# First mixer of a two-layer decoder trunk: seven block products in place of eight from the third channel block on

## The chip, the core and the metric

The kernel runs on one core of a Trainium2 chip. The metric is the device time of one execution in microseconds (us), from the first to the last instruction and what little lies around them; lower is better. The kernel before was timed three times: 1878.28, 1880.44 and 1884.79 us, a median of 1880.44 us.

## What is computed

The input x has 2048 positions of 1024 channels, in float32. The work, cut to what matters here:

```python
# layer 0: gated short convolution ("mixer")
h = rmsnorm(x, norm_a)
u = h @ w_in_a                                  # (2048,1024) @ (1024,4096)
B, C, X, G = split(u, 4)
y = B * conv3(C * X)                            # causal, width 3, per channel
x = x + (y * silu(G)) @ w_out_a
# shared keys and values, then layer 1: stick-breaking attention, 8 heads of 64
k, v = split(rmsnorm(x, norm_kv) @ w_kv, 2)
q, g = split(rmsnorm(x, norm_b) @ w_in_b, 2)
o = attention(q, k, v)                          # strictly causal, products of sigmoids, no softmax
x = x + (o * silu(g)) @ w_out_b
out = rmsnorm(x, norm_f)
```

## The kernel before

**Tiles.** x is held transposed and with its positions reversed (xT): channels lie on the 128 partitions, in KD = 8 blocks, and positions run along the free axis in 4 chunks c of CH = 512. Every product of a weight block with a chunk accumulates in one PSUM bank of 128x512.

**Three matmuls for one.** A float32 operand is split into a high part of type fp32r and a low part, the rest of it (`split`, L174: ScalarE casts the high part, VectorE or GpSimd subtracts it from the source). `mm3` (L203) multiplies high by high, high by low and low by high: 24 matmuls for an output block with the 8 channel blocks of the contraction.

**The mixer.** `mixer_in(cs)` (L277) loops over 8 output channel blocks cb, and for each over the chunks cs and the four gates C, X, B, G, so 4 x 24 matmuls for each cb and chunk. `mixer_in((0, 1))`, called m01, does the first two chunks together, so that each weight block is loaded and split once for both (`load_w`, L183, which also stores the split weights to DRAM for the chunks 2 and 3). Its normalisation is late: the matmuls run on x times the gain, and the factor 1/rms (`late_rms`, L250, tiles rs) is multiplied in behind them. Behind the matmuls of a chunk and cb: C is copied out by ScalarE (L318), multiplied with X (L325) and with the square of 1/rms (L331), put through the convolution (L338, L339, L341), multiplied with B (L343), and with the sigmoid of G, G itself and 1/rms (L348 to L354). The result goes to DRAM (y_d) and is fetched again by `proj_out`.

**Beside m01.** `stats_x` (L220) computes 1/rms of the chunks 2 and 3, 8 loads, 8 squares and 7 additions each. `fold_gains` (L360) goes through 16 blocks of the weights w_kv and w_in_b: each half block is loaded, multiplied by its gain (L368, VectorE), split (L176) and stored (L371).

**Order.** The program's generators (`mixer_in`, `proj_first`, `attention_chunk` and others) are merged by hand with weights (`merge`, `take`, the last lines of the kernel): m01 runs alone for a quarter of one chunk's work, then it is merged with the statistics and the folds, and afterwards the output projection of chunk 0 (`proj_out`, tiles po) is merged with the mixer of chunk 2, and so on. A list scheduler then puts the instructions into a fixed order on each engine; each engine runs its list in that order, and an instruction that waits holds what is behind it. DMAs are issued by SyncE (SP) in the same manner.

**Buffers.** Split weights lie in NWB = 4 tiles of 128 x 2 x 8 x 128 (whl), raw weights in NRAW = 2 tiles (wraw). The tags w, R, wth, wtl, q2, kt, vv, ot, hl and og belong to the attention and the projections, and are free or nearly free during m01.

Of the kernel before, what the change touches and what calls it, by code (L numbers as in the profile page):

```python
# [8 lines left out]
F32 = mybir.dt.float32  # L9
# [12 lines left out]
NR, NW, NT, NL, NWB, NRAW, NA, NWTS = 5, 8, 4, 5, 4, 2, 16, 2  # L22
# [7 lines left out]
NB = 3  # L30
GRP, GRY, SLACK = 3, 6, 8
# [14 lines left out]
def kernel(  # L46
# [117 lines left out]
    def square_into(acc, src, first, nm, eng=nc.vector, early=False):  # L164
        if first:
            nc.scalar.activation(acc, src, AF.Square)
        else:

            tag = "wth" if early else "t"
            sq = sb.tile([P, CH], F32, name=f"sq_{nm}", tag=tag, bufs=NT if tag == "t" else NWTS)  # L170
            nc.scalar.activation(sq, src, AF.Square)
            eng.tensor_add(acc, acc, sq)
# [5 lines left out]
    def w_tile(nm, kt=KD):  # L178
        return sb.tile([P, 2, kt, P], F32R, name=f"whl_{nm}", tag="whl", bufs=NWB)
# [4 lines left out]
    def load_w(src, key, nm, kt=KD, eng=nc.vector):  # L184

        if key not in split_d:
            wt = w_tile(nm, kt)
            raw = sb.tile([P, kt, P], F32, name=f"wr_{nm}", tag="wraw", bufs=NRAW)
            nc.sync.dma_start(out=raw, in_=src.rearrange("(k p) n -> p k n", p=P))
            split(wt[:, 0], wt[:, 1], raw, eng)  # L190
            split_d[key] = dram.tile([P, 2, kt, P], F32, name=f"sw_{nm}")
            nc.sync.dma_start(out=split_d[key], in_=wt.bitcast(F32))
            return wt
        wt = w_tile(nm, kt)
        nc.sync.dma_start(out=wt.bitcast(F32), in_=split_d[key])
        return wt
# [6 lines left out]
    def mm3(ps, wts, a, kt=KD):  # L203

        hi, lo = wts[:, 0], wts[:, 1]
        n = 0
        for k in range(kt):
            for w, m in ((hi, 0), (hi, 1), (lo, 0)):
                ins = nc.tensor.matmul(ps, w[:, k, :], a[k][:, m, :], start=n == 0, stop=n == 3 * kt - 1)  # L209
# [11 lines left out]
    def load_x(c, k, nm):  # L221
        x = ld512(f"x{nm}_{c}_{k}")
        nc.sync.dma_start(out=x, in_=xT[k * P:(k + 1) * P, cols(c)])
        return x

    def norm_x_late(c, between=None):

        hc, xs = [], []
        for k in range(KD):
            if k == 1 and between is not None:  # L230
                between()
            tag, bufs = (("w", NW), ("R", NR) if k < NR else ("ld", NL))[c]
# [11 lines left out]
    def squares(c, xs):  # L244
        acc = sb.tile([P, CH], F32, name=f"acc_h{c}", tag="acc", bufs=2)
        for k, x in enumerate(xs):
            square_into(acc, x, k == 0, f"h{c}{k}", nc.gpsimd, early=True)
        return acc

    def late_rms(c, y):  # L250
        pb = bcast(y, f"h{c}")
        r = sb.tile([P, CH], F32, name=f"rs_{c}", tag="w", bufs=NW)
        nc.scalar.copy(r, pb)
        r2 = sb.tile([P, CH], F32, name=f"rs2_{c}", tag="w", bufs=NW)
# [3 lines left out]
    rx = {}  # L258

    def stats_x(c):  # L260

        acc = sb.tile([P, CH], F32, name=f"acc_h{c}", tag="acc", bufs=2)
        for k in range(KD):
            square_into(acc, load_x(c, k, "s"), k == 0, f"h{c}{k}", early=True)
        y = const.tile([P, 4], F32, name=f"rx_{c}")
        rx[c] = rstd(acc, f"h{c}", y)
        yield 1.0

    def norm_x(c):
        hc = []  # L270
        pb = bcast(rx[c], f"hb{c}")
        for k in range(KD):
            x = load_x(c, k, "n")
# [8 lines left out]
    late_acc, late = {}, {}  # L282

    def mixer_in(cs):
# [3 lines left out]
        for cb in range(KD):  # L288
            wts = {}
            for c in cs:  # L290
# [5 lines left out]
                def gate(g, i):  # L296
                    if c not in h:
                        if c == 0:
                            load_first = lambda: wts.update({g: load_w(w_src(i), (g, cb), f"{g}{cb}_{cs[0]}")})
                            h[c], late_acc[c] = norm_x_late(c, load_first)  # L300
                        else:
                            h[c], xs = norm_x_late(c)
                            late_acc[c] = rstd(squares(c, xs), f"h{c}")
# [43 lines left out]
                if c in late:  # L347
                    nc.vector.tensor_mul(sg, pG, late[c][0])  # L348
                    nc.scalar.activation(sg, sg, AF.Sigmoid)
                    nc.vector.tensor_mul(t, t, late[c][1])  # L350
# [3 lines left out]
                nc.vector.tensor_mul(t, t, pG)  # L354
                nc.sync.dma_start(out=y_d[c][cb], in_=t)
                yield rest(24)


    def fold_gains():

        for nm, src, gain in (("kv", w_kv, gains["kv"]), ("b", w_in_b[0], gains["b"])):
            for i in range(KD):
                split_d[nm, i] = dram.tile([P, 2, KD, P], F32, name=f"sw_{nm}{i}")
                for j in range(0, KD, 4):
                    hi, lo = (sb.tile([P, 4, P], F32R, name=f"fold{m}_{nm}{i}_{j}", tag="og", bufs=KD) for m in range(2))
                    raw = lo.bitcast(F32)
                    nc.sync.dma_start(out=raw, in_=src[j * P:(j + 4) * P, i * P:(i + 1) * P].rearrange("(k p) n -> p k n", p=P))
                    nc.vector.tensor_mul(raw, raw, gain[:, j:j + 4].unsqueeze(2).to_broadcast([P, 4, P]))  # L368
                    split(hi, lo, raw)
                    for m, t in enumerate((hi, lo)):  # L370
                        nc.sync.dma_start(out=split_d[nm, i][:, m, j:j + 4, :], in_=t.bitcast(F32))  # L371
                yield 1.0
# [3 lines left out]
    def proj_out(c):  # L376

        y = []
        for k in range(KD):
            y.append(act_tile(f"y_{c}", k))  # L380
            t = ld512(f"yr_{c}_{k}")
# [27 lines left out]
    def proj_k(c, kb):  # L409
        wts = load_w(None, ("kv", kb), f"k{c}_{kb}")  # L410
# [9 lines left out]
    def proj_q(c, qb):  # L420
        wts = load_w(None, ("b", qb), f"q{c}_{qb}")
# [7 lines left out]
    def proj_v(c, vb):  # L429
        wts = load_w(None, ("kv", 4 + vb), f"v{c}_{vb}")  # L430
# [12 lines left out]
    def proj_g(c, gb):  # L443
        wts = load_w(None, ("b", 4 + gb), f"gg{c}_{gb}")
# [175 lines left out]
    def out_b_last(c):  # L620
# [3 lines left out]
        for ob in range(KD):  # L624
# [3 lines left out]
            yield from mm3(ps, wts, og, kt=3)  # L628
# [10 lines left out]
        for ob in range(KD):  # L639
            ps = lin(f"pol_{ob}")  # L640
            yield from mm3(ps, wl[ob // 4][:, :, ob % 4:ob % 4 + 1, :], og[3:4], kt=1)
# [88 lines left out]
    run(take(m01, TA / 4))  # L730
# [48 lines left out]
```

## Time and profile before

The page shows one execution, profiled.

| | |
|---|---|
| profiled execution, its own time | 1879.31 us |
| its span, first to last instruction | 1877.6 us |
| median of three runs | 1880.44 us |
| m01: its last matmul is followed by the first of `proj_out` at | 369.3 us |
| matmuls in the whole kernel, as the profile counts them | 8312 |
| mean granted TensorE clock | 0.979 |

In the rows below PE is TensorE's matmuls, PEld its weight loads, DVE VectorE, ACT ScalarE, POOL GpSimd and SP SyncE. A row of a group gives line, engine, operation, tiles and shape, then the count, the busy time in us with the mean of one in ns, and the idle time of that engine just before them. A row of the timeline gives start and duration in us. A row by windows gives the busy time of each engine in the stretch, then the granted clock, the busy share of the DMA engines, and GB/s.

### The profile page before, as it was taken

The page shows a single profiled execution, that of the slowest core. Times are in us where ns is not written, and L with a number is a line of the kernel's source. Part 1 is how long each engine was busy: PE and PEld are TensorE (multiplying, and loading weights), DVE is VectorE, ACT ScalarE, POOL GpSimd, SP SyncE. Part 2 cuts the span into 40 slices and gives each one's busy share as a digit, 9 for nine tenths or more (in the row PEclk, how much of TensorE's full clock was granted, in tenths as well). Part 3 has the DMA queues.
Part 4 walks back from the last instruction along what each step waited for, and adds up shares of the span by engine and source line. Part 5 has one row for each costly group of instructions (what it writes and reads, how often), then busy time and mean ns, then how long its engine had stood idle before and what let it go on. Part 6 is the DMA issues. An engine that isn't in the chain of part 4 may idle for free.

```text
span 1877.6 us, 24951 instructions
## 1 busy us (share of the span) xinstructions
PE 1771.9 (94%) x8312; PEld 1447.6 (77%) x8312; DVE 1261.9 (67%) x1927; ACT 772.7 (41%) x1497; POOL 450.4 (24%) x822
## 2 busy tenths in 40 slices
PE   7999999999999999999999999999988998988783
PEld 5888888888778878887888888888766886866562
DVE  7876534554243364478785478787858889889984
ACT  6423212231232143345443244454535556556642
POOL 5100000101111032132221122232223214547543
PEclk9999999999999999999999999999999999999896
DMA  9999865697978798867677766566586667778763
GB/s 292 309 324 332 307 195 165 209 328 280 336 250 281 227 330 257 290 207 250 216 253 244 248 195 204 183 215 198 180 300 196 223 194 265 260 238 278 225 196 130
DMA packets 238480, 460.44 MB, mean 245 GB/s; under 512 B 18448, under 2 KB 133136, under 8 KB 213776
## 3 DMA queue, kind: packets, MB, share of 16 engines
q1 hardware_dynamic: 178272, 400.09, 63.0%
q10 hardware_dynamic: 59920, 58.74, 10.9%
q8 instruction: 66, 1.08, 0.2%
q14 instruction: 62, 0.51, 0.1%
q0 software_dynamic: 160, 0.02, 0.1%
HBM read 322.73 MB, written 136.05 MB: 244 GB/s over the span
## 4 chain that ended last, share of the span: by engine, by line
PE 74%; DVE 10%; DMA 7%; issue 4%; ACT 2%; POOL 2%; SPq 0%; ACTq 0%; POOLq 0%; DVEq 0%
PE pX L209 9%; PE pB L209 9%; PE po L209 9%; PE pG L209 9%; PE pC L209 8%; PE wt L526 4%; PE pv L209 4%; PE pk L209 3%; PE pq L209 3%; DVE R L514 3%; PE pg L209 3%; PE av L536 3%; PE av L535 2%; PE z L500 2%; PE z L501 2%
## 5 line engine op out<-in xcount | busy, mean ns | idle before, releaser
L514 DVE TENSOR_TENSOR_SCAN R<-R,R,ones 128x512 f32<-128x512 f32 x192 | 255.0, 1330 | 25.2 <-ACT R L503 24.7
L503 ACT ACTIVATE R<-z 128x512 f32<-128x512 f32 (+1 forms) x320 | 174.0, 544 | 185.0 <-PE z L501 72.7
L176 DVE TENSOR_TENSOR wtl<-wt,wth 128x512 fp32r<-128x512 f32 (+1 forms) x320 | 186.2, 601 | 79.9 <-ACT wth L175 76.8
L175 ACT CAST wth<-wt 128x512 fp32r<-128x512 f32 (+1 forms) x320 | 159.6, 528 | 184.7 <-PE wt L526 150.3
L518 DVE TENSOR_TENSOR w<-w,R 128x512 f32<-128x512 f32 (+1 forms) x320 | 207.7, 658 | 19.6 <-POOL R L511 2.1
L209 PE MATMUL pC<-h,whl_C 128*128 128x512 f32 x768 | 189.8, 396 | 11.0 <-ACT whl_C L175 8.0
L513 POOL COPY R<-R 128x1 f32<-128x1 f32 x192 | 117.4, 613 | 340.9 <-DVE R L514 308.6
L209 PE MATMUL po<-y,whl_o 128*128 128x512 f32 x768 | 189.2, 393 | 2.4 <-DVE x L394 2.0
L209 PE MATMUL pX<-h,whl_X 128*128 128x512 f32 x768 | 186.3, 392 | 1.3 <-DVE cv L354 1.3
L209 PE MATMUL pB<-h,whl_B 128*128 128x512 f32 x768 | 185.9, 392 | 0.0
L209 PE MATMUL pG<-h,whl_G 128*128 128x512 f32 x768 | 185.7, 392 | 0.0
L526 PE MATMUL wt<-ident,w 128*128 128x128 f32 x1088 | 176.8, 278 | 7.5 <-DVE w L518 4.5
L209 PEld LDWEIGHTS pC<-h,whl_C 128*128 128x128 f32 x768 | 143.5, 189 | 44.1 <-ACT whl_C L175 8.0
L505 ACT ACTIVATE w<-z 128x512 f32<-128x512 f32 (+1 forms) x320 | 172.1, 543 | 2.5 <-PE wt L526 2.4
L209 PEld LDWEIGHTS pX<-h,whl_X 128*128 128x128 f32 x768 | 143.5, 188 | 31.5 <-DVE cv L354 1.5
L209 PEld LDWEIGHTS po<-y,whl_o 128*128 128x128 f32 x768 | 142.7, 188 | 32.1 <-DVE x L394 2.2
L209 PEld LDWEIGHTS pB<-h,whl_B 128*128 128x128 f32 x768 | 143.5, 188 | 29.7
L209 PEld LDWEIGHTS pG<-h,whl_G 128*128 128x128 f32 x768 | 143.6, 188 | 29.5
L526 PEld LDWEIGHTS wt<-ident,w 128*128 128x128 f32 x1088 | 137.4, 143 | 36.0 <-DVE w L518 6.9
L536 PE MATMUL av<-wtl,vv 128*128 128x512 f32 (+1 forms) x320 | 127.3, 401 | 27.0 <-DVE wtl L176 26.5
L514 DVE TENSOR_TENSOR_SCAN R<-R,ones 128x512 f32<-128x512 f32 (+3 forms) x128 | 116.4, 915 | 37.0 <-POOL R L509 32.8
L500 PE MATMUL z<-kt,q 128*128 128x512 f32 (+1 forms) x320 | 129.3, 406 | 5.7 <-ACT w L505 2.8
(172 smaller groups left out, 2685.1 us busy)
## 6 DMA issues: line engine op xcount, KB each, us to landing
whl_o<-sw_o SPq DMA_DIRECT2D x24, 1024.0 KB, 5.3
kt<-k_d ACTq DMA_DIRECT2D x80, 256.0 KB, 4.0
vv<-v_d ACTq DMA_DIRECT2D x80, 256.0 KB, 3.7
whl_C<-sw_C SPq DMA_DIRECT2D x16, 1024.0 KB, 5.9
whl_X<-sw_X SPq DMA_DIRECT2D x16, 1024.0 KB, 5.3
whl_B<-sw_B SPq DMA_DIRECT2D x16, 1024.0 KB, 5.8
whl_G<-sw_G SPq DMA_DIRECT2D x16, 1024.0 KB, 5.3
whl_k<-sw_kv SPq DMA_DIRECT2D x16, 1024.0 KB, 7.0
```

The costliest lines, as they stand in the source:

```text
L175: nc.scalar.copy(hi, src)
L176: eng.tensor_sub(lo, src, hi.bitcast(F32))
L209: ins = nc.tensor.matmul(ps, w[:, k, :], a[k][:, m, :], start=n == 0, stop=n == 3 * kt - 1)
L500: nc.tensor.matmul(ps[:, lom:CH], q2[:, 0, qi * P:(qi + 1) * P], kt[:, lom:CH], start=True, stop=False)
L501: nc.tensor.matmul(ps[:, lom:CH], q2[:, 1, qi * P:(qi + 1) * P], kt[:, lom:CH], start=False, stop=True)
L503: nc.scalar.activation(R[:, lo + 1:CH + 1], ps[:, lo:CH], AF.Sigmoid, scale=-0.125)
L505: nc.scalar.activation(w[:, lo:CH], ps[:, lo:CH], AF.Sigmoid, scale=0.125)
L513: nc.gpsimd.tensor_copy(R[:, 0:1], carry[qi])
L514: nc.vector.tensor_tensor_scan(out=R[:, lo + 1:CH + 1], data0=R[:, lo + 1:CH + 1], data1=ones[:, 0:1].to_broadcast([P, CH - lo]), initial= ...
L518: nc.vector.tensor_mul(w[:, lo:CH], w[:, lo:CH], R[:, lo:CH])
L526: nc.tensor.transpose(wt[:, qi * P:(qi + 1) * P], ws[qi][:, kb * P:(kb + 1) * P], ident)
L536: ins = nc.tensor.matmul(av[:, 0:n], vs, wl[:, 0:n], start=False, stop=final)
```

## The change

The channel blocks 0 and 1 of m01 (NPL = 2) stay as they were, except that 1/rms and not its square is multiplied in once for G and once for B, with a SiLU of ScalarE in place of sigmoid and product. From block 2 on, `mixer_fast` takes two gates at a time, C with X, and B with G: the 2x2 blocks are two gates, two halves of the contraction (Q = 4 channel blocks each) and two chunks. A "unit" is one cb and one pair of gates; there are 12 of them. Each does 7 products of 12 matmuls (three for each of 4 channel blocks) where there were 8, in the form of Strassen's scheme with 4 sums on each side:

- operands, once: both chunks of x are normalised in place (16 multiplications, L420 and L430), 16 differences are taken by GpSimd, and 7 operands of 4 tiles are split; the low parts of one of them (t4) by GpSimd, of the others by VectorE;
- weights, for each unit: 4 raw halves are loaded (L464), 4 sums and differences are formed, two by VectorE and two by GpSimd, and 8 half blocks are split, the low parts of two (s3, s4) by GpSimd;
- results, for each unit: four partial results are copied from PSUM by ScalarE (`keep`), and three additions by VectorE put the outputs together. The bank `fa` collects products 1, 2, 3 and the last one, with a copy in between.

```diff
-NR, NW, NT, NL, NWB, NRAW, NA, NWTS = 5, 8, 4, 5, 4, 2, 16, 2
+NR, NW, NT, NL, NWB, NRAW, NA, NWTS = 5, 8, 4, 5, 8, 4, 16, 2
...
+    def fast_operands():
+        x0, x1 = x_in[1], x_in[0]
...
+        operand("b11", x0[:Q], [(w2, w2)] * Q)
+        for k in range(Q):
+            nc.gpsimd.tensor_sub(x0[k], x1[k], x0[k])
...
+        operand("t1", x0[:Q], [(hs[2 * k], hs[2 * k + 1]) for k in range(Q)])
...
+    def fast_weights(n, cb, gs):
...
+            sp(key, raw)
...
+            if key == "a22":
+                nc.vector.tensor_add(a22, a21, a22)
+                sp("s1", a22)
+                nc.gpsimd.tensor_sub(a21, a11, a21)
+                nc.vector.tensor_sub(a11, a22, a11)
+                sp("s2", a11)
+        nc.gpsimd.tensor_sub(a12, a12, a11)
+        sp("s4", a12, nc.gpsimd)
+        sp("s3", a21, nc.gpsimd)
...
+            yield product(a, w["a11"], "b11", True, False)
+            c0 = keep(f"f1_{nm}", a)
+            yield product(d, w["s1"], "t1", True, False)
+            p5 = keep(f"f5_{nm}", d)
...
+                yield last_product(n - 1)
+            yield product(a, w["s2"], "t2", False, False)
+            c1 = keep(f"f2_{nm}", a)
+            yield product(d, w["s4"], "b22", False, True)
+            nc.vector.tensor_add(c1, c1, d)
...
+                yield product(c, w["a12"], "b21", True, True)
+                nc.vector.tensor_add(c0, c0, c)
+            yield product(a, w["s3"], "t3", False, False)
+            x1 = keep(f"f3_{nm}", a)
+            nc.vector.tensor_add(x1, x1, p5)
...
-    run(take(m01, TA / 4))
-    merge((m01, 1.75 * TA), (chain(iter((DLY,)), stats_x(2), stats_x(3), fold_gains()), 18.0 + DLY))
+    run(take(m01, TA / 2))
+    merge((m01, 1.3 * TA), (chain(iter((DLY,)), stats_x(2), stats_x(3), fold_gains([(n, i) for i in range(8) for n in ("kv", "b")]), stats_end()), 26.0 + DLY))
```

Split weights now lie in half blocks (8 tiles of half the size) everywhere, so each load, split and store of a full block is two instructions on halves. The statistics and the folds start after channel block 1, not within block 0, and their loads are tied to a matmul that precedes them (`follow`), so that they are spread over the stretch. The result of chunk 0 and block 7 is split on the spot (`y_last`) and does not go through DRAM.

More of the change, by code (lines that the diff above doesn't have):

```diff
@@ L287, in mixer_in @@
             yield YN * 24 * MM
-        for cb in range(KD):
+        for cb in range(KD if len(cs) == 1 else NPL):
             wts = {}
+            if cb == NPL - 1 and len(cs) > 1:
+                fast_operands()
             for c in cs:
```

271 lines of the change are left out of this document (217 added, 54 removed).

## The prediction

> **What bounds the kernel now.** I read the page first, then the stretches by windows, then the chain of work in order of time, and last what TensorE waited for.
>
> ```profile
> PE 1771.9 (94%) x8312; PEld 1447.6 (77%) x8312; DVE 1261.9 (67%) x1927; ACT 772.7 (41%) x1497; POOL 450.4 (24%) x822
> ```
> ```profile
> 28.00:106.40 78.40, 77.17 (x343) 63.68 (x344) 64.49 (x122) 35.45 (x55) 14.22 (x14) 1.00 0.92 317
> 106.40:369.40 263.00, 263.00 (x1169) 218.22 (x1169) 140.85 (x212) 65.72 (x91) 12.80 (x27) 1.00 0.75 250
> ...
> 1440.00:1877.60 437.60, 368.62 (x1743) 290.75 (x1741) 372.98 (x532) 240.31 (x470) 188.80 (x259) 0.93 0.69 222
> ```
> ```profile
> 100.96 5.44 PE pG L209 x24
> 106.40 5.44 PE pC L209 x24
> ...
> 363.99 5.44 PE pG L209 x24
> 369.43 5.45 PE po L209 x24
> ```
>
> TensorE is busy 94% of the span. The change touches the work of m01 alone, and m01 ends at 369.4 us, where the first matmul of the output projection (po) stands in the chain. Its channel blocks 0 and 1 are done at 106.4 us; from there to 369.4 us TensorE is busy in 263.00 of 263 us, at a granted clock of 1.00. The chain is nothing but outputs of 24 matmuls at 5.44 us each, 226.7 ns a matmul. In this stretch time is matmuls, and VectorE has slack: 140.85 us busy of 263.
>
> **The change part by part.** My sum is made against the profiled execution: 1879.31 us (span 1877.6), 1.1 us under the median of 1880.44, so I carry the same number over to the median.
>
> *TensorE.* The stretch had 6 blocks x 2 chunks x 4 gates x 24 = 1152 matmuls, and gets 12 units x 7 x 12 = 1008, on the same tile shapes, each with its own weight load as before. 144 fewer at 226.7 ns is **-32.6 us**: 228.5 us for the products instead of 261.1 (the rest of the 263 is statistics, which stay, so 231 in all). The rest of the program keeps its matmuls.
>
> *What VectorE gets in exchange.* Its durations:
>
> ```profile
> 42.56 1.22 DVE L176 TENSOR_TENSOR whl_G<-wr_G,whl_G 128x1024 fp32r<-128x1024 f32 x1
> 43.70 1.22 DVE L176 TENSOR_TENSOR whl_C<-wr_C,whl_C 128x1024 fp32r<-128x1024 f32 x1
> ...
> 49.70 0.75 DVE L341 SCALAR_TENSOR_TENSOR cv<-p,cw,cv 128x512 f32<-128x512 f32 x1
> 50.37 0.69 DVE L172 TENSOR_TENSOR acc_h<-acc_h,sq_h 128x512 f32<-128x512 f32 x1
> 50.97 0.68 DVE L343 TENSOR_TENSOR cv<-cv,pB 128x512 f32<-128x512 f32 x1
> 51.57 0.69 DVE L348 TENSOR_TENSOR sg<-pG,rs 128x512 f32<-128x512 f32 x1
> ```
>
> From start to start a 128x512 TENSOR_TENSOR takes 0.60 us, with a scalar as third input 0.67, and a 128x1024 one 1.14. A pair of units (one channel block) holds 12 low parts, 4 sums of weights, 6 additions of products, and 6 + 4 instructions of convolution and gating: 28 x 0.60 + 4 x 0.67 = 19.5 us, 117 us for six blocks. The folds and statistics, partly done before 106 us until now, fall into the stretch whole: 64 + 14 instructions, 46.8 us. Small ones for the statistics, and the first output weights and y ahead of po: some 13 us. Together **177 us** where 231 are to be had.
>
> *GpSimd, and its quarrel with VectorE.* The stretch gets 48 differences and low parts for the weights, 8 for t4 and 2 for y: 58 of 128x512. Before, such ones ran at the start of the kernel:
>
> ```profile
> 11.55 1.28 POOL L172 TENSOR_TENSOR acc_h<-acc_h,sq_h 128x512 f32<-128x512 f32 x1 [0.59 <-ACT sq_h L171]
> ...
> 26.07 8.75 POOL L172 TENSOR_TENSOR acc_h<-acc_h,sq_h 128x512 f32<-128x512 f32 x5 [0.27 <-ACT sq_h L171]
> ```
> ```profile
> 26.81 1.75 DVE L239 SCALAR_TENSOR_TENSOR h<-xh,g_a,h 128x512 fp32r<-128x512 f32 x1
> ...
> 29.09 2.89 DVE L239 SCALAR_TENSOR_TENSOR h<-xh,g_a,h 128x512 fp32r<-128x512 f32 x2
> ...
> 31.97 1.70 DVE L239 SCALAR_TENSOR_TENSOR h<-xh,g_a,h 128x512 fp32r<-128x512 f32 x1
> 33.60 1.25 DVE L134 TENSOR_SCALAR t_h<-v_h 128x4 int32<-128x4 int32 x1
> ```
>
> Alone, GpSimd takes 1.28 us. Five in a row beside a busy VectorE take 1.75 each, and VectorE's own, 0.75 us as at 49.70, take 1.75, 1.45 twice and 1.70; a tiny one of 128x4 takes 1.25. These five cost VectorE about 1.0 + 1.4 + 0.95 + 1.1 = 4.4 us, 0.9 each, though VectorE had work at every moment. I take **0.8** for one, since some will fall into VectorE's waits; the ends are 0 (all of them do) and 1.28 (each whole). 58 x 0.8 = 46 us, so VectorE needs 177 + 46 = **223 of 231 us**, 97%. GpSimd itself, at 58 x 1.75 = 102 us, is far from full.
>
> The Trainium skill's page "SBUF — State Buffer", section "Who interferes with whom", says that a VectorE instruction with two SBUF inputs and a GpSimd instruction that reads SBUF exclude each other, and that whoever comes second blocks until the other is through. The rows above agree as far as they go; taken to the letter it is the upper end of 1.28 us, and the second rival below is what that end gives.
>
> *How much TensorE waits.* At 97% the two engines are level, and each waits for the other by turns. Two stretches of before bracket it: from 28 to 106.4 us VectorE was 82% busy (64.49 of 78.40) and TensorE lost 1.2 us; from 1440 us on VectorE was 85% busy, and TensorE idle for 69 of 437.6 us (16%), above all for VectorE:
>
> ```profile
> PE av L536 <- DVE wtl L176: 24.1, 21, 2.7
> ```
>
> The second stretch is attention, with short steps to and fro; weights here are split about one unit (19 us) ahead, which is nearer to the first. I take a little over 4% of 231, **+10 us**; ends 0 and 16%, 37 us.
>
> *Entry.* VectorE can't normalise the second chunk before its rs is there:
>
> ```profile
> 67.20 0.69 DVE L331 TENSOR_TENSOR p<-p,rs 128x512 f32<-128x512 f32 x1 [1.91 <-ACT rs L255]
> ```
>
> In the changed order that is again before TensorE's 216th matmul or so. From there 57 instructions (35.1 us) and 13 of GpSimd's (10.4 us at 0.8) lie ahead of the last low part of b21, so 67.2 + 45.5 = 112.7 us. TensorE asks for b21 behind its first two products, at 106.4 + 5.4 = 111.8. That is 1 us late, with 0 and 1.28 for the contention from 0 to 7; I take **+2**.
>
> *Exit.* po's first matmul needs y_0, which VectorE splits behind y_7, and y_7 hangs on the last unit's third product.
>
> ```profile
> L349 ACT ACTIVATE sg<-sg 128x512 f32<-128x512 f32 x15 | 9.5, 630 | 28.9 <-DVE sg L348 28.9
> L318 ACT COPY cs<-pC 128x512 f32<-128x512 f32 x16 | 9.3, 581 | 26.0 <-PE pC L209 26.0
> ...
> L175 ACT CAST y<-yr 128x512 fp32r<-128x512 f32 x8 | 5.0, 622 | 6.3 <-PE pG L209 4.5 <-DMA yr<-y_d 1.5
> ```
>
> Copy, addition, SiLU, product, cast, low part, then y_0: 0.58 + 0.60 + 0.63 + 0.60 + 0.62 + 0.60 + 0.60 and 0.6 of small work is 4.8 us, of which the last product (12 matmuls, 2.7 us) hides 2.7. **+2**, ends 0 and 5 (two instructions of GpSimd's in the way).
>
> *At nothing.* ScalarE gets 16 weight casts, 8 copies, 2 scalings and 2 SiLUs a block, 28 x 0.62 = 17 of 38 us, and the folds' casts; TensorE's other products hide it unless ScalarE is held behind a late VectorE, which the +10 holds. The halved loads move the same bytes, but double SyncE's issues; each is prefetched, and another load in flight hides it.
>
> Sum: -32.6 + 10 + 2 + 2 = -18.6 us; 1879.3 - 18.6 = 1860.7, **1861 us**.
>
> **The rivals.**
>
> *All is hidden.* If contention falls into VectorE's waits (0 in place of 0.8: 177 of 231, 77% busy, less than the 82% that cost 1.2 us above), only TensorE's sum counts: 1879.3 - 32.6 = **1847**. For it: between 106.4 and 369.4 us nothing at all held TensorE. Against: the five instructions above.
>
> *VectorE becomes the bound, slower than before.* If each of the 58 costs VectorE its whole 1.28 us, that is 74, and 177 + 74 = 251 us. VectorE's list is fixed, and it also stands still for the folds' loads:
>
> ```profile
> DVE fold_b L368 <- DMA fold_b<-in_w_in_b_dram: 22.2, 13, 3.2
> ...
> DVE fold_kv L368 <- DMA fold_kv<-in_w_kv_dram: 4.6, 4, 2.1
> ```
>
> With 22 of these 27 us, VectorE takes 273, against the old 263: 1879.3 + 10 = **1889**. It decides from the price x at which 177 + 58x + 22 > 263, that is x = 1.1 us. Against: 0.9 measured with VectorE never free.
>
> *Late folds.* At 0.8, and with the folds' 27 us of waits on top of 223, VectorE needs 250, 19 more than TensorE; with entry and exit, -32.6 + 19 + 4 = -9.6: **1870**. The loads speak for it:
>
> ```profile
> xs<-in_xT_dram SPq DMA_DIRECT2D x16, 256.0 KB, 6.3
> fold_kv<-in_w_kv_dram SPq DMA_DIRECT2D x16, 256.0 KB, 6.2
> ```
> ```profile
> 35.49 0.68 DVE L368 TENSOR_TENSOR fold_kv<-fold_kv,g_kv 128x512 f32<-128x512 f32 x1
> ...
> 103.76 0.69 DVE L368 TENSOR_TENSOR fold_kv<-fold_kv,g_kv 128x512 f32<-128x512 f32 x1 [1.31 <-DMA fold_kv<-in_w_kv_dram]
> ```
>
> The stretch moved 250 GB/s x 263 us = 66 MB at a DMA share of 0.75. Some 11 MB of it that were moved before 106 us (16 loads for the statistics, 4 MB, and 9 half folds, the two rows above and seven between, of 0.75 MB with their stores) come in, 77 MB in 231 us, 330 GB/s; the stretch from 28 us on did 317 at 0.92. Against: the change paces those loads, and GpSimd's work that falls into these waits costs nothing.
>
> **How the numbers follow.** Forecast, 1852 to 1866 us: 0.45. All hidden: 0.20. Late folds: 0.20. VectorE the bound: 0.15. The range takes in all but the worse part of the last and the little below all hidden: 1845 to 1883. About 0.3% (5.6 us) is what a measurement of this kernel can tell from no change. Faster by more: 0.45 + 0.20 + 0.13 of the late folds = 0.78; within: the other 0.07; slower: 0.15.
>
> **What would show it.** In the changed profile the first po starts near 351 us (369.4 - 18.6); near 337 all was hidden, beyond 369 VectorE is the bound. In the Strassen stretch VectorE should be busy over 90%, its low parts of the weights should average 0.8 us or more instead of 0.69, and TensorE's waits should be many small ones, released by VectorE or by casts of ScalarE that follow it, 14 us in all; a matmul should still be 226.7 ns. Long waits of VectorE for fold loads would speak for the late folds. From po on the time should be as before, within 5 us; if it differs by more, the halved weight tiles or the new order there did something that I left out.

## The result and the profile after

The changed kernel takes **1910.58 us**, the median of four runs (1910.32 to 1919.14), beside 1882.62 us for the kernel before on the same chip (four runs, 1878.28 to 1889.84): a ratio of 1.0151, 95% interval 1.0124 to 1.0179. It is slower by about 28 us, where 1861 was forecast and the range ended at 1883. Its profiled execution is the longest of its four, 1919.14 us with a span of 1917.4, 8.6 us over the median; what is said of places goes by that execution.

First its page, the row of busy time:

```profile
PE 1773.5 (92%) x8168; PEld 1433.6 (75%) x8168; DVE 1346.4 (70%) x2039; ACT 834.3 (44%) x1650; POOL 552.1 (29%) x890
```

The 144 matmuls are gone (8168 for 8312), and yet TensorE is busy 1.6 us longer than before. The first matmul of the output projection (po) shows what became of the stretch; second row, the stretch by windows, from 106.4 us to there (PE, PEld, DVE, ACT, POOL busy, then clock, DMA share, GB/s):

```profile
L217 PE MATMUL po<-y,whl_o x115: 387/389/797, 382.8 to 419.7; 128*128 128x512 f32 x115
```
```profile
106.40:382.80 276.40, 248.78 (x1037) 196.67 (x1035) 218.82 (x315) 129.28 (x235) 104.76 (x83) 0.97 0.82 269
```

po starts at 382.8 us, not at 369.3 as before and not at 351 as forecast. VectorE's busy time, 218.82 us, is what I had worked out (223), but in 276 us and not in 231. TensorE is idle for 27.6 us there. What it waited for, and below it what ScalarE waited for in the same stretch (total, times, longest):

```profile
PE fa_C L489 <- ACT f_C L499: 8.0, 7, 2.1
PE fa_B L489 <- ACT f_B L499: 6.1, 7, 1.6
PE po L217 <- ACT y L176: 5.3, 1, 5.3
PE fd_B L489 <- ACT whl_s_B L176: 3.1, 1, 3.1
```
```profile
ACT fold_kv L176 <- DVE fold_kv L590: 22.2, 12, 4.0
ACT fold_b L176 <- DVE fold_b L590: 17.0, 9, 3.4
ACT whl_s_C L176 <- POOL fr_C L476: 13.3, 5, 4.3
ACT whl_s_B L176 <- POOL fr_B L476: 11.6, 5, 3.0
ACT sq_h L172 <- DMA xs<-in_xT_dram: 11.0, 6, 2.9
```

TensorE is not released by VectorE but by ScalarE, which is busy 129 of 276 us: its copy of a bank (`keep`, L499), or its cast, stands in its list behind casts that wait. They wait for three things: the folds (VectorE's product, which waits for a load), GpSimd's sums of weights, and the loads of the statistics. One chain in the timeline (start, duration), ScalarE and then TensorE:

```profile
172.17 0.61 ACT L176 CAST whl_a_B<-fr_B 128x512 fp32r<-128x512 f32 x1
177.50 0.63 ACT L169 ACTIVATE acc_h<-xs 128x512 f32<-128x512 f32 x1 [4.72 <-DMA xs<-in_xT_dram]
178.03 0.60 ACT L176 CAST whl_s_B<-fr_B 128x512 fp32r<-128x512 f32 x1
```
```profile
178.69 0.73 PE L489 MATMUL fd_B<-op_t,whl_s_B 128*128 128x512 f32 x2 [3.15 <-ACT whl_s_B L176]
179.26 4.54 PE L489 MATMUL fa_B<-op_b,whl_a_B 128*128 128x512 f32 x12
183.64 2.65 PE L489 MATMUL fa_C<-op_t,whl_s_C 128*128 128x512 f32 x11
```

A square of the statistics, which nobody needs for 200 us, waits 4.72 us for its load, and the cast that TensorE needs stands behind it. The row below the wait shows a second loss: 12 matmuls take 4.54 us in place of the usual 2.9.

And GpSimd beside VectorE, the rows of the changed stretch for the low parts and sums that each makes (count, busy us, mean ns), with the same sums on VectorE in the run below without GpSimd:

```profile
L177 POOL TENSOR_TENSOR whl_s_C<-fr_C,whl_s_C 128x512 fp32r<-128x512 f32 x12 | 19.7, 1658 | 4.0 <-ACT whl_s_C L176 4.0
L476 POOL TENSOR_TENSOR fr_C<-fr_C,fr_C 128x512 f32<-128x512 f32 x6 | 12.1, 2014 | 28.1 <-DVE whl_a_C L177 28.1
```
```profile
L177 DVE TENSOR_TENSOR fold_kv<-fold_kv,fold_kv 128x512 fp32r<-128x512 f32 x16 | 13.4, 840 | 1.4 <-ACT fold_kv L176 1.4
L177 DVE TENSOR_TENSOR whl_s_B<-fr_B,whl_s_B 128x512 fp32r<-128x512 f32 x12 | 10.5, 876 | 4.8 <-ACT whl_s_B L176 4.4
```
```profile
L476 DVE TENSOR_TENSOR fr_C<-fr_C,fr_C 128x512 f32<-128x512 f32 x6 | 4.1, 682 | 0.0
```

The same sum takes GpSimd 2014 ns and VectorE 682, and VectorE's own low parts grow from 0.69 to 0.84 and 0.88 us in the two groups shown (the other groups of low parts lie between 0.68 and 0.83, but for those of the operands at the entry, of which the last section speaks).

### The profile page after: what moved, and what is told of

The parts are those of the page before. It is cut to its first block, busy times and chain, and to the rows that moved or that the text cites. A ratio compares the mean times of both kernels' runs of the same rounds, so it can differ in the third digit from the quotient of the medians.

```text
span 1917.4 us, 25511 instructions
## 1 busy us (share of the span) xinstructions
PE 1773.5 (92%) x8168; PEld 1433.6 (75%) x8168; DVE 1346.4 (70%) x2039; ACT 834.3 (44%) x1650; POOL 552.1 (29%) x890
## 4 chain that ended last, share of the span: by engine, by line
PE 57%; DVE 14%; DMA 9%; issue 7%; POOL 3%; ACT 2%; SPq 1%; POOLq 0%; ACTq 0%; DVEq 0%
PE po L217 8%; PE pX L217 5%; PE wt L757 4%; PE pv L217 4%; PE pC L217 4%; PE pB L217 4%; PE pk L217 4%; PE pG L217 4%; PE pq L217 3%; DVE R L745 3%; PE pg L217 3%; PE av L767 3%; PE av L766 2%; PE z L731 2%; PE z L732 2%
## 5 line engine op out<-in xcount | busy, mean ns | idle before, releaser
L744 POOL COPY R<-R 128x1 f32<-128x1 f32 x192 | 107.3, 560 | 360.2 <-DVE R L745 317.4
L217 PE MATMUL pC<-h,whl_C 128*128 128x512 f32 x480 | 124.6, 402 | 10.4 <-ACT whl_C L176 6.8
L740 POOL TENSOR_SCALAR_AFFINE_SELECT R<-R 128x128 f32<-128x128 f32 x128 | 56.8, 444 | 267.7 <-ACT R L734 265.3
L731 PE MATMUL z<-kt,q 128*128 128x512 f32 (+1 forms) x320 | 128.7, 405 | 4.9 <-ACT w L736 4.7
L766 PE MATMUL av<-wth,vv 128*128 128x512 f32 (+1 forms) x320 | 122.5, 383 | 8.1 <-ACT wth L176 7.6
L217 PE MATMUL pX<-h,whl_X 128*128 128x512 f32 x480 | 122.6, 401 | 1.2 <-DVE whl_X L177 1.0
L732 PE MATMUL z<-kt,q 128*128 128x512 f32 (+1 forms) x320 | 120.1, 378 | 0.0
L217 PE MATMUL pG<-h,whl_G 128*128 128x512 f32 x480 | 118.8, 392 | 0.7 <-DVE qhl L177 0.7
L217 PE MATMUL pB<-h,whl_B 128*128 128x512 f32 x480 | 118.8, 392 | 0.0
L217 PEld LDWEIGHTS pC<-h,whl_C 128*128 128x128 f32 x480 | 90.4, 192 | 33.4 <-ACT whl_C L176 6.8
```

The costliest lines, as they stand in the source:

```text
L217: ins = nc.tensor.matmul(ps, wts[k // Q][:, w, k % Q, :], a[k][:, m, :], start=n == 0, stop=n == 3 * kt - 1)
L731: nc.tensor.matmul(ps[:, lom:CH], q2[:, 0, qi * P:(qi + 1) * P], kt[:, lom:CH], start=True, stop=False)
L732: nc.tensor.matmul(ps[:, lom:CH], q2[:, 1, qi * P:(qi + 1) * P], kt[:, lom:CH], start=False, stop=True)
L766: nc.tensor.matmul(av[:, 0:n], vs, wh[:, 0:n], start=first, stop=False)
```

## The experiments

The theory at the start: GpSimd's work holds VectorE up, and all lists with it (**theory A**). The rivals: the folds' loads are late and hold the lists (**B**); the halved weight tiles, not the stretch, lose the time (**C**). Each run is set beside runs of the kernel before on the same chip; po is the time of its first matmul, read in each run's own profile as above (382.8 in the changed kernel). An edit also lets the list scheduler order the lists anew, so that each run tests its edit together with the order that came of it.

### GpSimd's work to VectorE (e1, e6)

```diff
-            nc.gpsimd.tensor_sub(x0[k], x1[k], x0[k])
+            nc.vector.tensor_sub(x0[k], x1[k], x0[k])
...
-                nc.gpsimd.tensor_sub(a21, a11, a21)
+                nc.vector.tensor_sub(a21, a11, a21)
...
-        sp("s4", a12, nc.gpsimd)
+        sp("s4", a12)
```

> The changed kernel, with all of GpSimd's new work (16 differences and 4 low parts of operands, 48 differences and low parts of weights) done by VectorE. Theory A, the quarrel between GpSimd and VectorE holds the Strassen stretch: VectorE's instructions fall back to 0.69 us from 0.76 to 0.92, it gains 68 x 0.60 = 41 us of work and loses some 45 us of blocking, the entry (waits from 116 to 140 us) goes, and the first po comes 8 to 15 us earlier than in the changed kernel (382.8), time 1896 to 1903. Theory B, in-order lists on ScalarE and VectorE wait behind loads and behind each other: the entry shrinks by a few us, the rest stays, first po within 6 us of 382.8, time 1903 to 1914.

Measured: 1890.05 us, ratio 1.0027 (1.0011 to 1.0043), po at 362.6. The page and the stretch:

```profile
PE 1765.0 (93%) x8168; PEld 1430.6 (76%) x8168; DVE 1337.1 (71%) x2107; ACT 836.1 (44%) x1650; POOL 446.8 (24%) x822
```
```profile
106.40:362.60 256.20, 242.70 (x1043) 195.22 (x1042) 218.14 (x379) 131.35 (x237) 10.43 (x25) 0.99 0.89 289
```

VectorE does 68 instructions more (2107 for 2039), 46.6 us at 0.685, and yet is busy for 9.3 us less: 1337.1 us for 1346.4. So GpSimd's 68 had cost VectorE 55.9 us, 0.82 each, more than doing them itself, while each took GpSimd 1.4 to 2.0 us. These are single executions; e8 and e18 below, in which VectorE does the same work, show 1342.3 and 1341.1 us, which makes the price 0.75 and 0.76. Giving this work to GpSimd had relieved nothing and made its results late. This holds for A, beyond its range: po comes 20.2 us earlier, where 8 to 15 were expected.

In e6 only the operands' part of the edit is made (the weights' stay on GpSimd).

> The changed kernel with the operands' subtractions and low parts (20 of GpSimd's operations, in the entry) given to VectorE; the weights' (36 to 38 operations, two sums and two low parts in each of 12 units) stay on GpSimd. No GpSimd at all moved the first po from 382.8 to 362.6. If the quarrel over the port costs per operation, the entry's third of them is worth 20/58 of 20 us: the first po at 376. If it is the entry's waits (7 us of waiting at 116 to 140 us and 4 to 6 us of half clock behind them), 11 to 13 us of the 20 are there: the first po near 370. If it is the lists held in order behind GpSimd's weights, hardly anything: 380 or later.

Measured: 1907.9 us, ratio 1.0137 (1.0117 to 1.0158), po at 377.2: 5.6 of the 20.2 us come from the operands, the other 14.6 from the weights, nearest to a price per operation, as the first of the three expectations has it.

### The folds left out, with GpSimd (e2) and without (e5)

```diff
-    merge((m01, 1.3 * TA), (chain(iter((DLY,)), stats_x(2), stats_x(3), fold_gains([...]), stats_end()), 26.0 + DLY))
+    merge((m01, 1.3 * TA), (chain(iter((DLY,)), stats_x(2), stats_x(3), stats_end()), 10.0 + DLY))
```

> The changed kernel without the folds beside the first mixer: w_kv and w_in_b are multiplied and split where they are first used, in the projections. 64 instructions of VectorE (38 us), 32 casts of ScalarE and 96 DMAs leave the stretch. Theory B: the waits for fold loads (17.7 us on VectorE) and what is queued behind them go, TensorE's waits for copies (14 us) fall below 6 and the first po comes at 352 to 362 us. Theory A: VectorE has fewer instructions, GpSimd's still block it, the entry stays, first po at 365 to 375. In both the projections behind it take longer, so that the time tells less than the first po.

Measured: 1907.43 us, ratio 1.0121 (1.0096 to 1.0146), po at 362.1. It gains 20.7 us in the stretch, just outside the range that B gave (352 to 362) and well ahead of A's, and pays most of it when the weights are scaled at their first use.

> The changed kernel with all of GpSimd's new subtractions given to VectorE and the folds of the scaled weights left out of the mixer's stretch (each weight is then scaled when it is first used, later). The folds are VectorE, ScalarE and queue work beside 2070 units of matmul. If the two costs simply add (no GpSimd: first po at 362.6; no folds: 362.1 against 382.8), the stretch is then no longer bound by VectorE at all, and the first po comes at 343 to 350, near the 337 that 231 us of matmul would give. If both kernels only came back to the same bound by different ways (VectorE's list, held by ScalarE's copies), the first po stays near 360. Whole time: what is gained here is paid again in the projections, as without folds alone (about 25 us later), so 1880 to 1895.

Measured: 1895.28 us, ratio 1.0074 (1.0055 to 1.0092), po at 346.9.

```profile
106.40:346.90 240.50, 237.51 (x1041) 193.14 (x1039) 182.56 (x309) 114.39 (x204) 9.35 (x25) 1.00 0.64 209
```

With both gone TensorE is busy 237.51 of 240.5 us at a clock of 1.00: here is what the scheme itself saves. Both costs are real, and neither alone is the bound. The whole is no faster, since the folds are paid later.

### What it is in the folds (e11, e13, e14, e15, e16)

VectorE's time was the first guess. In e11 the folds' 32 multiplications (0.69 us each) go to ScalarE, GpSimd's new work stays on VectorE.

```diff
-                nc.vector.tensor_mul(raw, raw, gain[:, j:j + Q].unsqueeze(2).to_broadcast([P, Q, P]))
+                for q in range(Q):
+                    nc.scalar.activation(raw[:, q, :], raw[:, q, :], AF.Copy, scale=gain[:, j + q:j + q + 1])
```

> The changed kernel with GpSimd's new subtractions given to VectorE (1890.05 us, first po at 362.6), and the folds' multiplication by the gain taken from VectorE (32 of 0.8 us, some 26 us) and done by ScalarE in four pieces of 128 columns each. By the theory that VectorE's list is the bound of the stretch, whose 53 us of folds were worth 15.7 us there (362.6 to 346.9), half of them gives 7 to 9 us: first po at 353 to 356, the whole 1881 to 1884. If ScalarE's list, in which TensorE's copies stand, is the bound, its 128 more instructions make it later: first po at 365 or more, 1892 or more.

Measured: 1895.96 us, ratio 1.0062 (1.0043 to 1.008), po at 366.0, later than without the edit. The guess fell: VectorE has 19 us less to do (199.42 for 218.14) and nothing is won.

```profile
106.40:366.00 259.60, 242.94 (x1036) 193.00 (x1035) 199.42 (x344) 166.12 (x362) 8.72 (x25) 0.99 0.88 284
```
```profile
ACT fold_kv L591 <- DMA fold_kv<-in_w_kv_dram: 21.4, 14, 2.9
ACT fold_b L591 <- DMA fold_b<-in_w_in_b_dram: 18.8, 8, 3.9
```

ScalarE now shows the wait itself: 40 us for the folds' loads. So e13 issues them one block (two loads) earlier, with the multiplication back on VectorE.

```diff
+        ahead = loads(*blocks[0])
         for n, (nm, i) in enumerate(blocks):
...
+            got = ahead
+            if n + 1 < len(blocks):
+                ahead = loads(*blocks[n + 1])
+            for j, hi, lo in got:
```

> The changed kernel with GpSimd's new subtractions given to VectorE (1890.05 us, first po at 362.6), and each fold's loads issued one block (two loads) earlier. If the loads' landing holds the lists, ScalarE's wait of 44 us behind the folds' multiplication falls to under half, and the first po comes at 350 to 357; the whole at 1878 to 1886. If the DMA engines' traffic or the engines' own time is the bound, nothing changes: 360 to 365.

Measured: **1879.44 us**, ratio 0.9986 (0.9967 to 1.0005), po at 350.2. ScalarE's wait behind the folds' products falls from 44 us to 0.3, VectorE's for their loads from 18.5 to none; waits of ScalarE for the folds' stores, 13.3 us, come in part in their place. The first row is of e1, the second of e13:

```profile
ACT fold_b L176 <- DVE fold_b L590: 25.1, 11, 4.7
```
```profile
ACT fold_b L176 <- DMA sw_kv<-fold_kv: 7.0, 2, 5.5
```

VectorE is as busy as ever, 88% of the stretch, and the DMA engines busier than ever:

```profile
106.40:350.20 243.80, 238.31 (x1040) 193.14 (x1038) 214.75 (x369) 130.18 (x234) 14.27 (x25) 1.00 0.94 308
```

```profile
PE 1752.9 (94%) x8168; PEld 1421.9 (76%) x8168; DVE 1340.6 (72%) x2107; ACT 835.5 (45%) x1650; POOL 451.0 (24%) x822
```

This holds for B, and TensorE's busy time is 20.6 us shorter than in the changed kernel, for the same matmuls. The stretch now ends 19.1 us sooner than in the kernel before, and yet the whole is only 0.14% faster, which is not clear of no change: the rest is lost behind po.

Where e13 gains its 12.4 us over e1 is seen by counting the scheme's 1008 matmuls. At number 980 e1 is only 2.8 us behind (345.27 and 342.46 us). The other 9.6 come at the exit, TensorE first and then ScalarE in e1:

```profile
354.00 5.49 PE L489 MATMUL fa_B<-op_t,whl_a_B 128*128 128x512 f32 x12 [4.93 <-ACT f_B L499]
```
```profile
352.84 0.62 ACT L176 CAST fold_b<-fold_b 128x512 fp32r<-128x512 f32 x1 [3.89 <-DVE fold_b L590]
353.37 0.58 ACT L499 COPY f_B<-fa_B 128x512 f32<-128x512 f32 x1
```

The copy that the last product needs stands behind the cast of the last fold. TensorE waits 4.93 us for it, its last 12 matmuls take 5.49 us at half the clock, and a further wait of 2.38 follows. In e13 the last cast of a fold is done at 315 us and not at 353, so no fold stands at the exit. A kernel that ends its folds as early by another order, with its loads as late as in e1, was not run.

In e14 the folds' stores alone are left out of e1 (and the projections read another tile):

```diff
-                for m, t in enumerate((hi, lo)):
-                    nc.sync.dma_start(out=split_d[nm, i][:, m, j:j + Q, :], in_=t.bitcast(F32))
```

> The same kernel with the folds' stores left out (64 of 256 KB, some 16.8 of 74 MB in the stretch; the projections then read another weight's tile, so that the output is another): loads, multiplications, casts and low parts are all kept. If traffic is the bound, the first po comes at 348 to 354; if the folds' engine work or their loads' lateness is, at 358 to 363.

Measured: 1881.42 us, ratio 0.9978 (0.9965 to 0.9991), po at 350.7, the DMA share 0.77. By itself this run speaks for the traffic as the bound; but e13 carries all the traffic at a share of 0.94 and is as fast. What fits both is that the stores delay the loads: VectorE waited 9.7 us for them here and 18.5 with the stores, and an earlier issue does the same good. ScalarE still waits 36.6 us for the folds' products here, so the sum of such waits is not what counts; but the folds are through at 318 us, ahead of the exit, as in e13. Whether the loads were held on SyncE behind the stores or on the DMA engines was not told apart.

e15 joins e13's edit and e11's:

> No new work on GpSimd, the folds' loads a block earlier, and their multiplication on ScalarE. If late loads were what kept the multiplication on ScalarE from helping (366.0 with it), the first po comes at 348 to 354 now, earlier than with the loads alone. If ScalarE's list is too full for 128 more instructions, 362 or later.

Measured: 1880.94 us, ratio 0.9982 (0.9966 to 0.9998), po at 351.0. With the loads in time the multiplications do no harm on ScalarE, and no good (an earlier po than e13's was expected): VectorE was not the bound. In e16, e11 with late loads, the copies out of TensorE's banks are taken out of ScalarE's list (48 of them by VectorE's count of instructions, 2123 for 2075, and not 36):

```diff
-            nc.scalar.copy(t, ps)
+            nc.vector.tensor_copy(t, ps)
```

> No new work on GpSimd, the folds' multiplication on ScalarE (1895.96 us, first po at 366.0), and the 36 copies of the running sums out of TensorE's banks on VectorE in place of ScalarE (VectorE then has 196 + some 27 us of work again). If ScalarE's list, held by loads, is what keeps TensorE waiting for these copies, the waits for them (12.6 us) go and the first po comes at 352 to 358. If VectorE's list is as late, TensorE waits for it instead: 364 to 370.

Measured: 1880.6 us, ratio 0.9987 (0.9967 to 1.0006), po at 356.8, 9.2 us earlier than e11, while ScalarE waits as long as ever for the folds' loads (24.2 and 23.5 us). With e15, where ScalarE is busy for 164.91 of 244.6 us and po still comes at 351.0, this says that it is not ScalarE's time but the place of these copies in a list that waits.

### Both costs crossed (e17)

e13's earlier loads in the changed kernel, GpSimd's work kept.

> The changed kernel, GpSimd's new work kept, with the folds' loads one block earlier. If GpSimd's operations cost time of their own (VectorE's instructions held beside them), the 20 us between the two kernels stay: first po at 366 to 374, the whole 1893 to 1900. If they only made late lists later, the first po comes at 350 to 358, the whole at 1879 to 1886.

Measured: 1905.12 us, ratio 1.0115 (1.0087 to 1.0142), po at 371.9.

```profile
PE 1766.9 (93%) x8168; PEld 1427.8 (75%) x8168; DVE 1353.5 (71%) x2039; ACT 834.6 (44%) x1650; POOL 566.0 (30%) x890
```
```profile
L177 DVE TENSOR_TENSOR fold_kv<-fold_kv,fold_kv 128x512 fp32r<-128x512 f32 x16 | 17.1, 1080 | 0.4 <-ACT fold_kv L176 0.4
```

| po at (us) | loads late | loads early |
|---|---|---|
| GpSimd's work kept | 382.8 | 371.9 |
| given to VectorE | 362.6 | 350.2 |

The two causes add to within 1.5 us: GpSimd 20.2 or 21.7 us, late loads 10.9 or 12.4. By the whole times GpSimd's work costs 1.2 to 1.3% (1.0151 for 1.0027, 1.0115 for 0.9986) and the late loads about 0.4%, though with GpSimd's work kept the intervals overlap (e17 lies 5 us above the range that was expected of the whole). That the loads cost so nearly the same in both rows is in part chance, since they cost it in other places: with GpSimd's work kept, 7.4 of the 10.9 us lie ahead of matmul 980 (369.94 and 362.58 us), without it 2.8 of 12.4. VectorE is busier with GpSimd's help than without it: 1353.5 us here, 1340.6 in e13 with 68 instructions more, so that each of GpSimd's cost it (1353.5 - 1340.6 + 46.6) / 68 = 0.88 us.

### Behind the stretch: halves and queues (e3, e4, e7, e8, e9, e10, e12, e18)

The changed kernel with NPL = KD, so without the scheme but with all the rest:

> The changed kernel with all 8 channel blocks in the old form (no Strassen, 144 matmuls back), but with half tiles, paced folds, SiLU and the later start of the folds kept. If all of the loss comes from the Strassen stretch, first po near 369 us and time 1876 to 1886. If the other parts carry the loss behind the first mixer, first po near 369 and time 1890 to 1900.

Measured: 1899.54 us, ratio 1.0077 (1.0057 to 1.0098), po at 370.6. So what comes with the scheme loses about 14 us by itself, nearly all of it behind po: for that half of the loss **C** may hold, and the next run asks how much of it is the halves. The kernel before with the halved tiles alone (NWB 8, NRAW 4, w_tile and load_w of the changed kernel):

> The kernel before with half weight tiles alone (8 of half the size, two loads, splits and stores for one). Same bytes, twice the DMA issues. If the halves cost nothing: 1876 to 1886 us. If they carry the loss behind the first mixer (some 15 us in the changed kernel, most of it beyond 1440 us): 1892 to 1900.

Measured: 1893.75 us, ratio 1.0053 (1.0035 to 1.0071), po at 369.9. The halves alone lose 9.5 us, and nothing of it in the stretch. The profiled execution is the longest of e4's six (1900.62 us) and loses more than the median, 20.4 us behind po. Counted by matmuls done since po, it falls behind the kernel before in steps: 6.8 us between 1400 and 1440 us of that kernel's time, 8.6 between 1500 and 1550; of 6.3 near 510 all but 1.0 is made up again by 550. (The control e10 below, without the halves, also falls 4 us behind near 1430.) At the step of 8.6 us SyncE's queue in e4, what held it, and what that held:

```profile
1555.13 1.12 SPq L198 DMA_DIRECT2D wr_ob<-in_w_out_b_dram  x1
1565.62 0.32 SPq L202 DMA_DIRECT2D sw_ob<-whl_ob  x1
...
1569.89 0.42 SPq L575 DMA_DIRECT2D ogr<-og_d  x1
```
```profile
SPq L202 <- POOL whl_ob L178: 9.3, 1, 9.3
```

SyncE stood 9.3 us at a store of output weights whose low part GpSimd had not made, and the next load of attention's output (ogr) behind it; in the kernel before the same wait is 3.0. The list is another one, perhaps since twice the raw tiles can be in flight; no run shows that reason. e7 puts that store on GpSimd's queue:

```diff
-                nc.sync.dma_start(out=split_d[key][:, :, j:j + Q, :], in_=wt.bitcast(F32))
+                (nc.gpsimd if eng is nc.gpsimd else nc.sync).dma_start(out=split_d[key][:, :, j:j + Q, :], in_=wt.bitcast(F32))
```

> The kernel before with the halved weight tiles alone (1893.75 us, 9.5 over before), and with the first use's store of the output weights, whose low parts GpSimd makes, put on GpSimd's own queue in place of SyncE's. If SyncE held 9.3 us behind GpSimd in that store is what loses 9 us at 1555 to 1570, this loss goes: 1884 to 1886, and the losses near 510 and 1430 stay. If the store only happened to stand where the loss is, nothing changes: 1892 to 1896. GpSimd's list then holds the stores' issue, which may cost its own work (each issue some tenths of a us, 8 of them).

> The changed kernel with all of GpSimd's new subtractions given to VectorE (1890.05 us) and the same store on GpSimd's queue. By the first theory the loss of 9 us at 1555 to 1570 goes: 1880 to 1882, a little below the kernel before. By the second: 1888 to 1892.

Measured: 1895.68 us, ratio 1.0075 (1.006 to 1.009), and 1893.58, ratio 1.0053 (1.0026 to 1.0079). Neither gained: e7 falls into its second range, e8 lies 1.6 us above its own. The profile of e7 shows why: SyncE now stands at the instruction behind it, the raw load into a tile that GpSimd has to free.

```profile
SPq L198 <- POOL whl_ob L178: 10.4, 1, 10.4
```

e9 moves that raw load too, in the same way, and the store of the values (v_d) to ScalarE's queue; near 510 us that store stood on SyncE behind halves waiting for TensorE. e10 is its control.

> The kernel before with halved weight tiles (1893.75 and, with the output weights' store alone on GpSimd's queue, 1895.68 us). Now both the raw load and the store of the output weights go on GpSimd's queue (with the store alone SyncE was held 10.4 us by the raw load of the fifth block, whose buffer GpSimd frees), and the stores of the values v_d go on ScalarE's queue (on SyncE, the halves' loads stand ahead of them and wait for TensorE; at 501 us the store was issued 3.3 us later than in the kernel before, and TensorE waited 4.6 for 1.3). If SyncE's list, held by the halves, is the whole cost of the halves, the 9 us at 1555 to 1570 and the 3 to 6 us near 510 and 1430 go: 1882 to 1886. If the cost is elsewhere (more transfers, ScalarE's later loads), 1891 to 1896.

> A control: the kernel before with only the stores of the values v_d on ScalarE's queue. TensorE waits there 1.3 and 3.7 us at 500 and 1410 for the cast that this store holds up. If the store was held by SyncE's list there too, 2 to 4 us are gained: 1877 to 1881; if it only lasts, no change. A loss would say that the store holds ScalarE's list.

Measured: e9 1888.88 us, ratio 1.0023 (1.0008 to 1.0038); e10 1883.74, ratio 0.9999 (0.9983 to 1.0015). e10 is no change. In e9 SyncE no longer waits for GpSimd near 1570, TensorE's wait near 510 is 2.0 us for 5.0, and about half of the 9.5 us is back; the intervals of e4 and e9 overlap by a little, so that this is likely and not settled. The rest was not found. Two runs put the remedies on Strassen's kernel, e12 with e11's edit and e9's, and e18 with e13's and e9's:

> All remedies at once on the changed kernel: no new work on GpSimd, the folds' multiplication on ScalarE, the output weights' raw loads and stores on GpSimd's queue, the values' stores on ScalarE's. If they add (7 to 9 us of the folds, 8 to 10 of the halves from 1890.05), 1872 to 1876, and so faster than the kernel before by 6 to 10. If the folds go wrong on ScalarE, 1882 or more; if the queues do not help, 1881 to 1884.

> The best kernel so far (no new work on GpSimd, the folds' loads a block earlier: 1879.44 us) with the output weights' raw loads and stores on GpSimd's queue and the values' stores on ScalarE's. These were worth 4.9 us on the kernel with halves alone. If they add: 1872 to 1877, faster than the kernel before beyond its spread; if not, 1878 to 1883.

Measured: e12 1897.83 us, ratio 1.007 (1.005 to 1.009), the case in which the folds go wrong on ScalarE (po at 365.8: e11's fault was still in it). e18 **1876.26 us**, ratio 0.9966 (0.9947 to 0.9986), po at 350.2, the fastest of all versions and faster than the kernel before by 0.34%. Whether the queues add to e13 is not settled, since the intervals overlap.

## Why the prediction was wrong, step by step

**TensorE, -32.6 us: right.** 144 matmuls fewer, and in e5, with both costs gone, po comes 22.4 us earlier. Of the missing 10, 3.2 are a later start (the scheme's first product at 109.42 us for 106.23), 3.0 are waits, and 4 are not accounted for.

**VectorE's own work and GpSimd's price, 223 us: right in size.** 218.82 measured; the price of one was 0.75 to 0.82 us, 0.88 with loads in time, forecast 0.8. But I added it to VectorE's sum without setting it beside the 0.685 that VectorE itself takes. The row that said so stood in the prediction (0.9 us by the five instructions). The Trainium skill's "SBUF — State Buffer", section "Who interferes with whom", has a mechanism that fits, an exclusive lock; its letter would be 1.28, and the measured price lies between a half and seven tenths of that.

**"I take a little over 4% of 231, +10 us": this is the step that failed.** It read TensorE's waits from VectorE's busy share. In e13 VectorE is 88% busy and po comes at 350.2; that this is nearly the 351 of the forecast is chance, since the forecast was for a kernel with GpSimd's work in it. In the changed kernel it is busy for 79% of the stretch, and TensorE loses 27.6 us idle and, measured against e5's 237.51 us for the same matmuls, 11.3 us more in matmuls at a lower clock. What decides here is not how full an engine is but how late the inputs are that its list waits for, and what stands behind. The signs that I had named failed with it: VectorE over 90% busy, 14 us of waits, a matmul at 226.7 ns throughout.

**Late folds and GpSimd as alternatives: wrong.** The rival had the right place (10.9 to 12.4 us against its 9 over the forecast), but I argued that "GpSimd's work that falls into these waits costs nothing". The crossed runs show that the two add: 350.2 + 12.4 + 21.7 is 384.3, and 382.8 was measured. And the loads do their harm not by filling VectorE's time, as the rival had it, but through ScalarE's list, in which TensorE's copies stand behind the folds.

**VectorE as the bound, 1889: not this mechanism.** The price stayed under 1.1 us, and the kernel is slower all the same, without VectorE being full.

**Entry +2, exit +2: too small.** TensorE's waits between 116 and 140 us come to 7 us, the end of my range, and the slow clock follows them; by the scheme's matmul 100 the changed kernel is 9.2 us behind e1 (143.09 and 133.87 us). At the exit it waits 5.35 us, not for GpSimd but for ScalarE's y, which stands behind a cast of output weights:

```profile
379.50 0.62 ACT L176 CAST whl_o<-wr_o 128x512 fp32r<-128x512 f32 x1 [5.15 <-DMA wr_o<-in_w_out_a_dram]
```

**"At nothing": the other step that failed, twice.** ScalarE's copies were to be hidden by other products, and held TensorE for 14.1 us. The halves cost 9.5 us by themselves (e4), though "another load in flight hides it": SyncE's list runs in order, and an issue that waited 9.3 us held the loads behind it. At most about half of the 9.5 us is traced to that.

**"From po on within 5 us": wrong.** Span less po is 1534.6 us for 1508.3 in the profiled executions, 26 longer (14.5 by the medians: 1910.58 - 382.8 against 1882.62 - 369.3). Of the 26, TensorE's busy time makes 15 (1429.69 us for 1414.60, with the same 6740 matmuls, at a granted clock of 0.96 for 0.97); idle time is the rest. I had named the cause (the halved tiles or the new order); it deserved a price, and had none.

## What to carry to other kernels

Before work goes to GpSimd, set its price for VectorE beside what VectorE would need itself: here 0.75 to 0.88 us against 0.685, so nothing was relieved, and each operation took two to three times as long. Where lists run in order, ask of every instruction that fills a gap what stands behind it, whether its load is surely there, and whether the filling ends before the part that is in a hurry: issuing the folds' loads a block earlier, with not one instruction fewer, brought po 12.4 us forward and the whole by 0.4%, about 8 us. And a change of buffer sizes is a change of every queue: price it alone.

## What the hardware showed that was not expected

**A few us of waiting cost several more at half the clock.** At the entry TensorE waits 0.67, 0.73, 1.64 and 1.38 us within 7 us, and in the last of these waits the clock falls; then, in the changed kernel, by windows of 2 us (PE busy, clock, DMA share, GB/s):

```profile
122.00:124.00 2.00, 1.01 (x2) 0.50 0.00 0
124.00:126.00 2.00, 2.00 (x6) 0.50 0.00 0
126.00:128.00 2.00, 2.00 (x6) 0.50 0.00 0
128.00:130.00 2.00, 2.00 (x9) 0.80 0.94 280
130.00:132.00 2.00, 2.00 (x11) 1.00 0.87 274
```

```profile
122.99 5.49 PE L489 MATMUL fa_C<-op_t,whl_s_C 128*128 128x512 f32 x12 [1.38 <-ACT f_C L499]
```

Twelve matmuls take 5.49 us, though no single wait was over 1.64 us. Read in windows of 0.4 us, the clock is 0.50 from 121.95 to 128.8 us here, from 180.0 to 183.4 behind the wait of 3.15 us that ends at 178.69, and from 381.4 to 391.6 at the exit: 6.8, 3.4 and 10.2 us, that is two, one and three times 3.4 us. The second begins more than 1 us after the matmuls have started again. The Trainium skill's "TensorE: Matmul & The Clock Gate", Part 1, "What's actually happening", has the half rate after an idle window of some 3.4 us and the full rate after as much sustained work; the factor and the steps of 3.4 us agree, while here a row of shorter waits was enough.

**Both sides pay where VectorE and GpSimd meet.** The same moments of the changed kernel, VectorE and then GpSimd:

```profile
120.09 0.68 DVE L375 TENSOR_TENSOR sg<-pG,rs 128x512 f32<-128x512 f32 x1
120.69 4.51 DVE L177 TENSOR_TENSOR op_t<-xh,op_t 128x512 fp32r<-128x512 f32 x3
```
```profile
117.89 3.40 POOL L444 TENSOR_TENSOR xh<-xh,xh 128x512 f32<-128x512 f32 x2
121.26 1.71 POOL L177 TENSOR_TENSOR whl_s_C<-fr_C,whl_s_C 128x512 fp32r<-128x512 f32 x1
...
124.62 6.36 POOL L177 TENSOR_TENSOR op_t<-xh,op_t 128x512 fp32r<-128x512 f32 x4
```

Three of VectorE's subtractions of two SBUF tiles take 4.51 us, and four of GpSimd's 6.36; the product just before, which reads PSUM (pG), takes 0.68 beside GpSimd as it does alone. Over the whole stretch it is the same for two additions of equal size, the first with both inputs in SBUF, the second with one in PSUM (fd_B):

```profile
L569 DVE TENSOR_TENSOR f_B<-f_B,f_B 128x512 f32<-128x512 f32 x6 | 6.6, 1096 | 1.6 <-ACT f_B L499 1.6
L563 DVE TENSOR_TENSOR f_B<-f_B,fd_B 128x512 f32<-128x512 f32 x6 | 4.1, 677 | 0.0
```
